# First up projection in 2x2 block products over half of the k-range, and modulation dots in the down projection

## The chip, the cores and the metric

The kernel runs on one core of a Trainium2 chip. A time is the device time of one execution in microseconds (us). The engines are TensorE (PE: matmuls; its weight loads are listed as PEld), VectorE (DVE), ScalarE (ACT), GpSimd (POOL) and SyncE (SP, which only issues transfers here). Transfers run on 16 DMA engines and are issued from the queues of SP, ACT and POOL.

## What is computed

One layer over 256 latent and 256 context tokens of width 2048, in f32: a half-step SwiGLU feed-forward (hidden width 5632) on both streams, token mixing (attention and a Hyena branch side by side), and a second half-step SwiGLU on the latent stream. Shift, scale and gate of each part come from a linear map of SiLU(c), nine chunks of 2048 columns each. Cut to what matters here:

```python
def swiglu(h, w_up, w_down):
    gate, up = jnp.split(h @ w_up, 2, axis=-1)
    return (jax.nn.silu(gate) * up) @ w_down

def half_ffn(s, m, slot, g, w_up, w_down):
    h = modulate(rms_norm(s, g), chunk(m, 3 * slot), chunk(m, 3 * slot + 1))
    return s + 0.5 * chunk(m, 3 * slot + 2) * swiglu(h, w_up, w_down)

mod   = silu(c)     @ w_ada + b_ada      # nine chunks, latent
mod_c = silu(c_ctx) @ w_ada + b_ada      # the same map, context
x   = half_ffn(x,   mod,   0, g_norm[0], w_ffn1_up, w_ffn1_down)
ctx = half_ffn(ctx, mod_c, 0, g_norm[0], w_ffn1_up, w_ffn1_down)
```

## The kernel before

**Tiles.** Activations are kept transposed: a k-tile is 128 features on the partitions and, on the free axis, 256 latent and 256 context tokens (2 x 256). There are 16 k-tiles of the width (KT) and 44 column tiles of the hidden width (JT; a column tile is called j). For precision every operand is split in two f32r parts, hi and lo, and `mm3` (L235) issues three matmuls for each product: hi x hi, hi x lo, lo x hi.

**Weights.** `weight` (L219) loads a raw tile of 128 x 1024 f32 (512 KB) from SP's queue into one of four "raw" slots, casts it to hi on ACT (L225) and subtracts to lo on DVE (L229). There are three slots each for hi ("whi") and lo ("wlo"). A raw slot is free once lo is made, a hi or lo slot once the last matmul that reads it is through.

**First up projection.** The first three j (WAVE) run beside the making of h. For j = 3 to 43 `Ffn.up` takes four pieces, one per quarter of the k-range: 4 k-tiles x (gate, up) x 3 matmuls of 512 columns. Two PSUM banks hold gate and up of one j; `close` (L372) applies SiLU on ACT, multiplies on DVE, splits the result and writes it to DRAM from POOL's queue. The h of all 16 k-tiles stays in SBUF in "u" tiles, 58 of which exist.

**Dots.** Chunk columns 2 to 8 of the modulation are made on DVE: `ada_dve` (L130) loads 128 columns x 1024 inputs (512 KB, four "adaw" slots, on SP's queue behind the newest weight load) and reduces them against SiLU(c) (L142); for chunks 2, 3 and 4 twice, with the context's as well. There are 7 x 16 x 2 = 224 such loads. After each piece a hook adds ADA_RATE = 1.375 to an account, and for each whole unit one load with its dots is issued. All are done when the up projection ends.

**First down projection.** `Ffn.down` (L414) makes three passes over 11 groups of four j: pass 0 and 1 with three double output tiles each, pass 2 with two. A step is one weight tile: 24 matmuls of 512. The act tiles of a group are fetched from DRAM on POOL's queue (`fetch`, L388) two groups ahead, up to five groups at a time; groups 9, 10 and 8 (the first of pass 0) are still in SBUF from the up projection. The last three groups of pass 2 are taken twice, with one half of the tokens each: 24 matmuls of 256 a step, context first, and the norm of the next stage runs beside the second half. The gate (chunk 2) is applied at the end of each pass.

The order of the instructions on each engine is written down when the program is built: a scheduler takes what is ready in its own estimate of times, earlier program text first, and each engine then runs its queue in that order.

Of the kernel before, what the change touches and what calls it, by code (L numbers as in the profile page):

```python
# [18 lines left out]
P = 128  # L19
D = 2048  # L20
# [11 lines left out]
WAVE = 3  # L32
ADA_RATE = 1.375
GT = JT // GRP
PASSES = ((0, 1, 2), (3, 4, 5), (6, 7))
ORDERS = ((9, 10, 8, 7, 6, 5, 4, 3, 2, 1, 0), tuple(range(GT)), tuple(reversed(range(GT))))
ROOM = 5
# [22 lines left out]
def hybrid_layer_kernel(ctx: ExitStack, tc: tile.TileContext, a):  # L60
# [288 lines left out]
    class Ffn:  # L349
        def __init__(self, wup, wdown, cm, hook=None):  # L350
            self.wup, self.wdown, self.cm = wup, wdown, cm
            self.hook = hook or (lambda: None)
            self.h = [None] * KT
            self.mm = mm3
            self.held = {}

        def open(self, alt=False):
            f = PB if alt else PA
            return f((P, 2, L)), f((P, 2, L))

        def piece(self, j, kq, ps2, w=None):
            w = w or weight(self.wup[j, kq], (P, 4, 2, P))
            for k4 in range(4):
                self.tile(kq * 4 + k4, k4, w, ps2)
            self.hook()

# [5 lines left out]
        def close(self, j, ps2):  # L372
            sg = tmp2((P, 2, L))
            S.activation(sg, ps2[0], AF.Silu)
            V.tensor_mul(sg, ps2[1], sg)
            act = split(sg, (P, 2, L))
            for s_ in range(2):
                nc.gpsimd.dma_start(actd[j][:, s_], act[s_])
            if j // GRP in ORDERS[0][0:3]:
                self.held.setdefault(j // GRP, []).append(act)  # L380

        def up(self, j, w=None):
            ps2 = self.open()
            for kq in range(4):
                self.piece(j, kq, ps2, None if kq else w)
            self.close(j, ps2)

# [25 lines left out]

        def down(self, before, between, after):  # L414

            uses = [(p, g) for p in range(len(PASSES)) for g in ORDERS[p]]
            for n, (p, g) in enumerate(uses):
# [17 lines left out]
                for dq in PASSES[p]:  # L435
                    self.hook()
                    self.step(g, dq, banks, g == ORDERS[p][0], g == ORDERS[p][-1] or at == -1)
            before()
            rest = [g for _, g in uses[-APART:]]
            for part in (1, 0):  # L440
# [5 lines left out]
                if part:  # L446
                    between()

# [113 lines left out]

    todo = [(c, d, b) for c in (2, 4, 3, 5, 7, 6, 8) for d in range(KT) for b in range(2)]
    owed = [0.0]

# [8 lines left out]
    def ada_hook():  # L574
        owed[0] += ADA_RATE
        while owed[0] >= 1.0:
# [193 lines left out]
    for _ in steps:  # L770
        pass
    ahead = weight(f1.wup[WAVE, 0], (P, 4, 2, P))
    for j in range(WAVE):
# [5 lines left out]

    xs = [[None] * (KT // 2) for _ in range(2)]  # L780
    for j in range(WAVE, JT):
        f1.up(j, ahead if j == WAVE else None)
        if j == WAVE:
            for i in range(2):
                crow.append(T(adap, (P, D), f"crow{i}", bufs=1))
                nc.scalar.dma_start(crow[i], a["crow"][i : i + 1, :].partition_broadcast(P))
                S.activation(crow[i], crow[i], AF.Silu)
            f1.hook = ada_hook
    while done[0] < len(todo):
        ada_next()  # L790
# [25 lines left out]
    f1.hook = lambda: None  # L816
    rs1 = U((P, 2, L))
    cont, lat = [], []

    def mix_input(i, out, early=None, bank=None):  # L820
        yield from rstd_steps(xs[i], D, rs1[:, i, :], early, bank)
        yield from normed_from(i, rs1[:, i, :], 3, out)

    more = mix_input(1, cont, PASSES[-1][0], PA)
    norm_plan = iter(NORM_PLAN)
    f1.down(lambda: next(more), lambda: next(more), lambda: [next(more) for _ in range(next(norm_plan))])


# [563 lines left out]
def _prepare(i):  # L1392
# [30 lines left out]
    d["cond"] = np.concatenate([pcol(i["b_ada"][0]).reshape(P, 9, KT), gn, cs], axis=1)  # L1423
    d["w_up1"] = pair(i["w_ffn1_up"][0], JT)
    d["w_dn1"] = down(i["w_ffn1_down"][0])
# [44 lines left out]
```

## Time and profile before

| | us |
|---|---|
| runs: median (lowest to highest) of 3 | 2661.37 (2660.85 to 2666.46) |
| the profiled execution | 2655.78 |
| its span, first to last instruction | 2653.9 |
| j = 4 to 43 of the first up projection | about 177 to 1050 |
| first down projection, pass 0 / 1 / 2 / the last steps | 1050 to 1230 / to 1410 / to 1497 / to 1532 |

The profile is of one execution; times in it are counted from the start of the span. A group's row has line, engine, operation, written and read tile, shapes and count, then the busy time and the mean duration of one in ns, then the idle time before it and what ended it. A matmul's record runs on after the next one has started, so its cost in a stream is read from the starts.

### The profile page before, as it was taken

Reading aid. Unit: us, or ns where it says so; the run is one execution under the profiler, and the core shown is the slowest. Engines: PE = TensorE matmul, PEld = TensorE weight load, DVE = VectorE, ACT = ScalarE, POOL = GpSimd, SP = SyncE. Lnnn points to the kernel's source line nnn. Section 1 sums busy time; section 2 is a strip of 40 time slices with the busy share of each in tenths; the row PEclk is TensorE's granted clock in tenths of the full one; section 3 lists DMA queues with packets and bytes.
Section 4 is the critical chain, followed back from the end, with each engine's and each line's share of the span. In section 5 each row is a group of like instructions: output and inputs, shape, how many; then the busy total and the mean of one; then the engine's idle time right before and its main releaser. Section 6 shows DMA issues by size and latency. Waiting matters only on the chain.

```text
span 2653.9 us, 32545 instructions
## 1 busy us (share of the span) xinstructions
PE 2630.5 (99%) x12434; PEld 2165.2 (82%) x12434; DVE 1606.4 (61%) x2393; ACT 930.4 (35%) x1208; POOL 152.8 (6%) x292
## 2 busy tenths in 40 slices
PE   8999999999999999999999999999999999999999
PEld 5678888788888888888888988888788888888887
DVE  6789999876665665223223496889665555554444
ACT  5332222222222222212112365456554444444333
POOL 1100000000000001410202100000000000000000
PEclk9999999999999999999999999999999999999999
DMA  9977767787777778953746555334555555556664
GB/s 366 362 263 254 253 237 263 232 282 258 253 258 248 260 251 273 345 159 127 224 133 209 190 172 191 122 132 162 173 182 191 190 190 189 188 188 206 204 199 159
DMA packets 178999, 579.75 MB, mean 218 GB/s; under 512 B 20635, under 2 KB 23644, under 8 KB 174492
## 3 DMA queue, kind: packets, MB, share of 16 engines
q1 hardware_dynamic: 139724, 500.72, 55.2%
q0 software_dynamic: 38496, 74.20, 9.5%
q10 hardware_dynamic: 624, 2.75, 0.3%
q8 instruction: 97, 1.59, 0.2%
q14 instruction: 58, 0.48, 0.1%
HBM read 550.32 MB, written 27.28 MB: 218 GB/s over the span
## 4 chain that ended last, share of the span: by engine, by line
PE 89%; DVE 5%; DMA 4%; issue 2%; ACT 0%; SPq 0%; DVEq 0%; ACTq 0%
PE pa L236 13%; PE pa L238 13%; PE pa L237 13%; PE pa L1132 10%; PE pa L1133 10%; PE pa L1134 10%; PE pb L236 3%; PE pb L237 3%; PE pb L238 3%; PE pa L244 3%; DMA adaw<-in_w_adaT_dram 2%; PE pa L246 2%; DVE adas L142 2%; DVE wlo L229 1%; PE pb L179 1%
## 5 line engine op out<-in xcount | busy, mean ns | idle before, releaser
L229 DVE TENSOR_TENSOR wlo<-raw,whi 128x1024 fp32r<-128x1024 f32 x637 | 779.4, 1224 | 793.3 <-ACT whi L225 769.7
L225 ACT CAST whi<-raw 128x1024 fp32r<-128x1024 f32 x637 | 670.0, 1052 | 1276.3 <-PE pa L237 561.4
L236 PE MATMUL pa<-u,whi 128*128 128x512 f32 (+1 forms) x1776 | 688.9, 388 | 2.1 <-ACT u L677 2.1
L238 PE MATMUL pa<-u,wlo 128*128 128x512 f32 (+1 forms) x1776 | 686.8, 387 | 2.2 <-DVE wlo L229 2.2
L237 PE MATMUL pa<-u,whi 128*128 128x512 f32 (+1 forms) x1776 | 686.7, 387 | 0.4 <-DVE u L682 0.4
L1132 PE MATMUL pa<-whi,u 128*128 128x512 f32 x1060 | 413.9, 391 | 0.0
L1133 PE MATMUL pa<-wlo,u 128*128 128x512 f32 x1060 | 412.8, 390 | 0.2 <-DVE wlo L229 0.2
L1134 PE MATMUL pa<-whi,u 128*128 128x512 f32 x1060 | 412.8, 390 | 0.0
L236 PEld LDWEIGHTS pa<-u,whi 128*128 128x128 f32 x1776 | 333.5, 188 | 75.2 <-issue 4.5
L238 PEld LDWEIGHTS pa<-u,wlo 128*128 128x128 f32 x1776 | 333.9, 188 | 70.9 <-DVE wlo L229 3.2
L237 PEld LDWEIGHTS pa<-u,whi 128*128 128x128 f32 x1776 | 333.9, 188 | 67.9 <-DVE u L682 1.5
L142 DVE CUSTOM_DVE_ANT_0 adas<-adaw,crow,cond 128x1024 bf16<-128x1024 f32 x160 | 205.2, 1282 | 51.3 <-DMA adaw<-in_w_adaT_dram 49.2
L142 DVE CUSTOM_DVE_ANT_0 adas<-adaw,crow,mod 128x1024 bf16<-128x1024 f32 x160 | 205.4, 1284 | 50.5 <-DMA adaw<-in_w_adaT_dram 47.3
L1134 PEld LDWEIGHTS pa<-whi,u 128*128 128x128 f32 x1060 | 199.0, 188 | 41.6
L1133 PEld LDWEIGHTS pa<-wlo,u 128*128 128x128 f32 x1060 | 199.1, 188 | 41.3 <-DVE wlo L229 0.6
L1132 PEld LDWEIGHTS pa<-whi,u 128*128 128x128 f32 x1060 | 199.0, 188 | 40.6
L236 PE MATMUL pb<-u,whi 128*128 128x512 f32 (+1 forms) x384 | 146.2, 381 | 0.0
L237 PE MATMUL pb<-u,whi 128*128 128x512 f32 (+1 forms) x384 | 144.5, 376 | 0.0
L238 PE MATMUL pb<-u,wlo 128*128 128x512 f32 (+1 forms) x384 | 144.4, 376 | 0.0
L244 PE MATMUL pa<-u,whi 128*128 128x512 f32 x384 | 137.4, 398 | 0.0
L395 POOL DMA_DIRECT2D u<-act x160 | 84.8, 550 | 337.7 <-PE pb L238 161.3
L246 PE MATMUL pa<-u,wlo 128*128 128x256 f32 x360 | 101.6, 283 | 0.0
(297 smaller groups left out, 2016.7 us busy)
## 6 DMA issues: line engine op xcount, KB each, us to landing
raw<-in_w_up_dram SPq DMA_DIRECT2D x340, 512.0 KB, 3.3
adaw<-in_w_adaT_dram SPq DMA_DIRECT2D x223, 512.0 KB, 5.6
raw<-in_w_dn_dram SPq DMA_DIRECT2D x182, 512.0 KB, 4.1
u<-act POOLq DMA_DIRECT2D x160, 256.0 KB, 6.1
wrow<-in_w_ada_dram SPq DMA_DIRECT2D x32, 1024.0 KB, 10.0
act<-u POOLq DMA_DIRECT2D x88, 256.0 KB, 5.4
raw<-in_w_hy_dram SPq DMA_DIRECT2D x32, 512.0 KB, 3.2
raw<-in_w_o_dram SPq DMA_DIRECT2D x32, 512.0 KB, 3.3
```

Of the source, the lines that this page charges most:

```text
L142: V.tensor_tensor_reduce(out=sc, in0=t, in1=crow[i][:, b * (D // 2) : (b + 1) * (D // 2)], scale=1.0, scalar=mcol if b else bada[:, n : n ...
L225: S.copy(hi, raw)
L229: V.tensor_sub(lo, raw, hi.bitcast(F32))
L236: PE.matmul(ps, w[0], xx[0], start=start, stop=False)
L237: PE.matmul(ps, w[0], xx[1], start=False, stop=False)
L238: return PE.matmul(ps, w[1], xx[0], start=False, stop=stop)
L244: PE.matmul(ps, w[0], x, start=start, stop=stop)
L246: PE.matmul(ps[:, 0, :], w[1], x[:, 0, :], start=False, stop=False)
L395: nc.gpsimd.dma_start(act[s_], actd[j][:, s_])
L1132: PE.matmul(ps[t], hi, w[0], start=start, stop=False)
L1133: PE.matmul(ps[t], hi, w[1], start=False, stop=False)
L1134: last = PE.matmul(ps[t], lo, w[0], start=False, stop=stop)
```

## The change

In the up projection the last quarter of the k-range is blocked from j = 4 on and the third quarter from j = 5 on (QUADS). A block product treats two k-tiles by two halves of the tokens (latent, context), and two k-tiles by gate and up, as 2x2 matrices and forms their product with seven products instead of eight. `combine` makes the sums and differences of h once for each pair of k-tiles and overwrites h's context half of the first k-tile; `prepare` makes those of the weights for each piece, in the raw tile, after the first three blocks are split (a tile of 768 columns) and before the other four are (1024 columns). A block piece is thus 2 pairs x 7 products x 3 = 42 matmuls of 256 columns. A j has four PSUM banks then, PA or PB in turn, and the end of `up` puts them together before SiLU.

The weights of j >= 3 lie in memory with their blocks in another order. The act tiles of the last groups are not kept in SBUF; the first group of the down projection is fetched during j = 43, the others in the usual way. Dots of chunks 5, 7, 6 and 8 are issued in the up projection (two loads a piece for j = 4 and 5, 0.7 a piece after that), those of chunks 2, 3 and 4 in the down projection, 1.27 loads a step. The pool that holds their tiles is given back after pass 2, and the constants of the mixing stage are loaded behind it.

```diff
@@ -30,10 +30,13 @@
 CT = HW // P
 EPS = 1e-6
 WAVE = 3
-ADA_RATE = 1.375
+ADA_UP = (5, 7, 6, 8)
+ADA_DOWN = (2, 3, 4)
+ADA_RATES = (2.0, 0.7, 1.27)
+QUADS = {3: 4, 2: 5}
 GT = JT // GRP
 PASSES = ((0, 1, 2), (3, 4, 5), (6, 7))
-ORDERS = ((9, 10, 8, 7, 6, 5, 4, 3, 2, 1, 0), tuple(range(GT)), tuple(reversed(range(GT))))
+ORDERS = ((9, 8, 10, 7, 6, 5, 4, 3, 2, 1, 0), tuple(range(GT)), tuple(reversed(range(GT))))
 ROOM = 5
 APART = 3
 NORM_PLAN = (0, 1, 0, 1, 0, 1, 1, 1, 1, 1, 1, 1)
@@ -353,16 +356,12 @@
             self.h = [None] * KT
             self.mm = mm3
             self.held = {}
+            self.sums = {}
+            self.wupq = a["w_up1q"]
 
         def open(self, alt=False):
             f = PB if alt else PA
             return f((P, 2, L)), f((P, 2, L))
-
-        def piece(self, j, kq, ps2, w=None):
-            w = w or weight(self.wup[j, kq], (P, 4, 2, P))
-            for k4 in range(4):
-                self.tile(kq * 4 + k4, k4, w, ps2)
-            self.hook()
 
         def tile(self, k, k4, w, ps2):
             for half in range(2):
@@ -373,17 +372,90 @@
             sg = tmp2((P, 2, L))
             S.activation(sg, ps2[0], AF.Silu)
             V.tensor_mul(sg, ps2[1], sg)
-            act = split(sg, (P, 2, L))
+            self.keep(j, sg)
+
+        def combine(self, kp):
+
+            (h0, l0), (h1, l1) = self.h[2 * kp], self.h[2 * kp + 1]
+            a0, a1, b0, b1 = tmp((P, 2, L)), tmp((P, 2, L)), tmp2((P, 2, L)), tmp2((P, 2, L))
+            V.tensor_add(a0, h0.bitcast(F32), l0.bitcast(F32))
+            V.tensor_add(a1, h1.bitcast(F32), l1.bitcast(F32))
+            V.tensor_add(b0[:, 0, :], a0[:, 1, :], a1[:, 1, :])
+            V.tensor_sub(b1[:, 0, :], b0[:, 0, :], a0[:, 0, :])
+            V.tensor_sub(b1[:, 1, :], a0[:, 1, :], a0[:, 0, :])
+            V.tensor_sub(b0[:, 1, :], a1[:, 0, :], b1[:, 0, :])
+            s23, s4 = split(b1, (P, 2, L)), U((P, 2, L), F32R)
+            split_to(b0[:, 0, :], h0[:, 1, :], l0[:, 1, :])
+            split_to(b0[:, 1, :], s4[:, 0, :], s4[:, 1, :])
+            self.sums[kp] = [(h0[:, 0, :], l0[:, 0, :]), (h1[:, 0, :], l1[:, 0, :]), (s4[:, 0, :], s4[:, 1, :]),
+                             (h1[:, 1, :], l1[:, 1, :]), (h0[:, 1, :], l0[:, 1, :]),
+                             tuple(t[:, 0, :] for t in s23), tuple(t[:, 1, :] for t in s23)]
+
+        def quads(self, j, kq):
+            return j >= QUADS.get(kq, JT)
+
+        def prepare(self, j, kq):
+
+            if not self.quads(j, kq):
+                return [weight(self.wupq[j - WAVE, kq], (P, 2, 4, P))]
+            raw = weight_load(self.wupq[j - WAVE, kq], (P, 2, 4, P))
+            out = []
+            for n in (3, 4):
+                if n == 4:
+                    V.tensor_sub(raw[:, :, 0:4:3], raw[:, :, 3:4].broadcast_to((P, 2, 2, P)), raw[:, :, 0:3:2])
+                    V.tensor_sub(raw[:, :, 2], raw[:, :, 2], raw[:, :, 0])
+                    V.tensor_sub(raw[:, :, 1], raw[:, :, 1], raw[:, :, 2])
+                hi, lo = T(wp, (P, 2, n, P), "whi", F32R, 3), T(wp, (P, 2, n, P), "wlo", F32R, 3)
+                out.append(split_to(raw[:, :, 0:n], hi, lo))
+            return out
+
+        def products(self, j, kq):
+
+            if not self.quads(j, kq):
+                for k4 in range(4):
+                    for half in range(2):
+                        yield half, None, 0, k4 // 2, (0, 1, 3, 2)[k4 % 2 + 2 * half], 4 * kq + k4
+                return
+            for n, terms in enumerate((((2, 0, 0, 0), (0, 0, 1, 1), (1, 0, 2, 2)),
+                                       ((0, 1, 1, 3), (3, 1, 0, 4), (2, 1, 2, 5), (3, 0, 3, 6)))):
+                for q in range(2):
+                    for bank, part, block, term in terms:
+                        yield bank, part, n, q, block, (2 * kq + q, term)
+
+        def up(self, j, w=None):
+            todo = [list(self.products(j, kq)) for kq in range(4)]
+            left = [sum(t[0] == bank for piece in todo for t in piece) for bank in range(4)]
+            total = list(left)
+            banks = [(PA, PB)[j % 2]((P, 2, L)) if n else None for n in left]
+            for kq in range(4):
+                w = w or self.prepare(j, kq)
+                for bank, part, n, q, block, x in todo[kq]:
+                    ps = banks[bank] if part is None else banks[bank][:, part, :]
+                    xx = self.h[x] if part is None else self.sums[x[0]][x[1]]
+                    left[bank] -= 1
+                    mm3(ps, [t[:, q, block] for t in w[n]], xx, left[bank] == total[bank] - 1, left[bank] == 0)
+                w = None
+                if j == JT - 1 and kq == 1:
+                    self.fetch(ORDERS[0][0])
+                self.hook()
+            if not total[2]:
+                return self.close(j, banks)
+            g, v, u = tmp((P, 2, L)), tmp2((P, 2, L)), T(up, (P, L), "mt", bufs=3)
+            S.copy(g[:, 0, :], banks[2][:, 0, :])
+            V.tensor_add(u, g[:, 0, :], banks[2][:, 1, :])
+            V.tensor_add(g[:, 1, :], u, banks[3][:, 0, :])
+            V.tensor_add(v[:, 0, :], u, banks[3][:, 1, :])
+            V.tensor_add(v[:, 1, :], g[:, 1, :], banks[3][:, 1, :])
+            V.tensor_add(g, g, banks[0])
+            V.tensor_add(v, v, banks[1])
+            S.activation(g, g, AF.Silu)
+            V.tensor_mul(v, v, g)
+            self.keep(j, v)
+
+        def keep(self, j, act):
+            act = split(act, (P, 2, L))
             for s_ in range(2):
                 nc.gpsimd.dma_start(actd[j][:, s_], act[s_])
-            if j // GRP in ORDERS[0][0:3]:
-                self.held.setdefault(j // GRP, []).append(act)
-
-        def up(self, j, w=None):
-            ps2 = self.open()
-            for kq in range(4):
-                self.piece(j, kq, ps2, None if kq else w)
-            self.close(j, ps2)
 
         def fetch(self, g):
 
@@ down @@
-        def down(self, before, between, after):
+        def down(self, after):
 ...
-            before()
+            yield
             rest = [g for _, g in uses[-APART:]]
 ...
                 if part:
-                    between()
+                    yield
 ...
@@ -560,8 +632,8 @@
                     yield
 
 
-    todo = [(c, d, b) for c in (2, 4, 3, 5, 7, 6, 8) for d in range(KT) for b in range(2)]
-    owed = [0.0]
+    todo = [(c, d, b) for c in ADA_UP + ADA_DOWN for d in range(KT) for b in range(2)]
+    owed, rate = [0.0], [0.0]
 
     def ada_next():
         if done[0] < len(todo):
@@ -572,7 +644,7 @@
                 ada_finish(c, d, d + 1)
 
     def ada_hook():
-        owed[0] += ADA_RATE
+        owed[0] += rate[0]
         while owed[0] >= 1.0:
             owed[0] -= 1.0
             ada_next()
@@ -769,7 +841,7 @@
                 raws = [weight_load(f1.wup[j, d // 4 + 1], (P, 4, 2, P), G) for j in range(WAVE)]
     for _ in steps:
         pass
-    ahead = weight(f1.wup[WAVE, 0], (P, 4, 2, P))
+    ahead = f1.prepare(WAVE, 0)
     for j in range(WAVE):
         f1.close(j, wave[j])
     rowp_cm.__exit__(None, None, None)
@@ -778,14 +850,31 @@
     crow = []
 
     xs = [[None] * (KT // 2) for _ in range(2)]
+    ready = {j: kq for kq, j in QUADS.items()}
     for j in range(WAVE, JT):
+        if j in ready:
+            for kp in (2 * ready[j], 2 * ready[j] + 1):
+                f1.combine(kp)
         f1.up(j, ahead if j == WAVE else None)
+        rate[0] = ADA_RATES[j >= 5]
         if j == WAVE:
             for i in range(2):
                 crow.append(T(adap, (P, D), f"crow{i}", bufs=1))
                 nc.scalar.dma_start(crow[i], a["crow"][i : i + 1, :].partition_broadcast(P))
                 S.activation(crow[i], crow[i], AF.Silu)
             f1.hook = ada_hook
+    rs1 = U((P, 2, L))
+    cont, lat = [], []
+
+    def mix_input(i, out, early=None, bank=None):
+        yield from rstd_steps(xs[i], D, rs1[:, i, :], early, bank)
+        yield from normed_from(i, rs1[:, i, :], 3, out)
+
+    more = mix_input(1, cont, PASSES[-1][0], PA)
+    norm_plan = iter(NORM_PLAN)
+    rate[0] = ADA_RATES[2]
+    downs = f1.down(lambda: [next(more) for _ in range(next(norm_plan))])
+    next(downs)
     while done[0] < len(todo):
         ada_next()
     last_load[0] = None
@@ after the kspec loads @@
-    more = mix_input(1, cont, PASSES[-1][0], PA)
-    norm_plan = iter(NORM_PLAN)
-    f1.down(lambda: next(more), lambda: next(more), lambda: [next(more) for _ in range(next(norm_plan))])
+    next(more)
+    next(downs)
+    next(more)
+    for _ in downs:
+        pass
 ...
@@ -1421,7 +1504,10 @@
     d["w_ada1"] = np.stack([w.reshape(2, 8, P, 2 * P).transpose(0, 2, 1, 3) for w in blocks])
     gn = i["g_norm"][0].reshape(3, KT, P).transpose(2, 0, 1)
     d["cond"] = np.concatenate([pcol(i["b_ada"][0]).reshape(P, 9, KT), gn, cs], axis=1)
-    d["w_up1"] = pair(i["w_ffn1_up"][0], JT)
+    w = pair(i["w_ffn1_up"][0], JT)
+    d["w_up1"] = c_(w[:WAVE])
+    w = w[WAVE:].reshape(JT - WAVE, 4, P, 2, 4, P)
+    d["w_up1q"] = c_(w[:, :, :, :, [0, 2, 3, 1], :])
     d["w_dn1"] = down(i["w_ffn1_down"][0])
     w = i["w_ffn2_up"][0].reshape(8, 2, P, 2, UPG, 256)
     d["w_up2"] = c_(w.transpose(4, 0, 2, 1, 3, 5)).reshape(UPG, 8, P, 2, 512)
```

More of the change, by code (lines that the diff above doesn't have):

```diff
@@ L816, in hybrid_layer_kernel @@
     f1.hook = lambda: None
[L817 to L822, printed above, removed]
-    more = mix_input(1, cont, PASSES[-1][0], PA)
-    norm_plan = iter(NORM_PLAN)
-    f1.down(lambda: next(more), lambda: next(more), lambda: [next(more) for _ in range(next(norm_plan))])
+    next(more)
[3 more added lines that the diff above has]
+        pass
     def proj_cols(w, ttiles, hook=lambda: None):
```

## Prediction

> **What bounds the kernel now.** I read the page first, then the windows by stage, then the order of single instructions in one stage.
>
> ```profile
> span 2653.9 us, 32545 instructions
> PE 2630.5 (99%) x12434; PEld 2165.2 (82%) x12434; DVE 1606.4 (61%) x2393; ACT 930.4 (35%) x1208; POOL 152.8 (6%) x292
> ...
> PE   8999999999999999999999999999999999999999
> PEld 5678888788888888888888988888788888888887
> DVE  6789999876665665223223496889665555554444
> ...
> PE 89%; DVE 5%; DMA 4%; issue 2%; ACT 0%; SPq 0%; DVEq 0%; ACTq 0%
> ```
>
> The reader is to see that TensorE (PE) is busy in every slice and makes 89% of the chain that ended last: time goes only if TensorE gets less work, and comes back if it has to wait. VectorE (DVE) is the next: nine tenths in slices 4 to 7, six tenths in the rest of the first up projection, two in the down projection (slices 17 to 22).
>
> ```profile
> 160.00:420.00 260.00, 260.00 (x1148) 215.29 (x1148) 239.13 (x399) 65.92 (x74) 13.36 (x26) 1.00 0.77 260
> 177.40:1050.00 872.60, 870.44 (x3839) 720.05 (x3838) 648.82 (x970) 210.17 (x240) 42.65 (x80) 1.00 0.76 256
> 1050.00:1230.00 180.00, 180.00 (x796) 149.10 (x795) 46.69 (x46) 37.12 (x37) 41.34 (x78) 1.00 0.69 222
> 1080.00:1110.00 30.00, 30.00 (x134) 24.84 (x133) 6.70 (x6) 5.28 (x5) 11.90 (x23) 1.00 1.19 388
> 1498.00:1514.00 16.00, 16.00 (x136) 16.00 (x135) 8.51 (x10) 5.96 (x7) 0.00 (x0) 1.00 0.49 165
> ```
>
> These are windows: length, busy PE, weight loads, DVE, ACT, POOL, granted clock, DMA share, GB/s. From 160 to 420 us DVE is 92% busy (239.13 of 260) and PE loses nothing. In the whole stretch of column tiles j = 4 to 43 (177.4 to 1050) PE lacks 2.2 us, and the waits (engine, what it waited for, us in all, times, longest) name them:
>
> ```profile
> PE pa L238 <- DVE wlo L229: 2.2, 2, 1.3
> DVE adas L142 <- DMA adaw<-in_w_adaT_dram: 96.5, 85, 3.8
> ```
>
> **Step 1, the products.** Two sets of starts on PE: matmuls 512 wide in the up projection (first and last of 57), and 256 wide at the end of the down projection (first and last of 24, the shape of the new block products).
>
> ```profile
> 214.69 0.39 PE L237 MATMUL pa<-u,whi 128*128 128x512 f32 x1
> ...
> 227.38 0.39 PE L236 MATMUL pa<-u,whi 128*128 128x512 f32 x1
> ...
> 1514.44 0.28 PE L236 MATMUL pb<-u,whi 128*128 128x256 f32 x1
> ...
> 1517.20 0.28 PE L238 MATMUL pb<-u,wlo 128*128 128x256 f32 x1
> ```
>
> A 512-wide matmul costs 12.69 / 56 = 0.2266 us, a 256-wide one 2.76 / 23 = 0.120 us: more than half. An old piece (a quarter of the k-range of one j) is 4 k-tiles x 2 halves x 3 = 24 matmuls of 512: 5.44 us. A block piece is 2 pairs x 7 products x 3 = 42 of 256: 5.04 us. The eighth saved becomes 7%: 0.40 us. The last quarter is blocked from j = 4 (40 pieces), the third from j = 5 (39): 79 x 0.40 = **31.6 us less**. The margin is thin: at 5.44 / 42 = 0.1295 us a matmul the gain is gone.
>
> Weight loads (PEld) rise from 24 to 42 a piece. In the window 1498 to 1514 they are busy 16.00 of 16.00 us, and the spacing is still 0.120 there, so I take 0.120. [...]
>
> **Step 2, the added VectorE and ScalarE work.** Durations of one, by shape:
>
> ```profile
> L229 DVE TENSOR_TENSOR wlo<-raw,whi 128x1024 fp32r<-128x1024 f32 x637 | 779.4, 1224 | 793.3 <-ACT whi L225 769.7 <-DMA adaw<-in_w_adaT_dram 7.4 <-DMA u<-in_xT_dram 4.2
> L142 DVE CUSTOM_DVE_ANT_0 adas<-adaw,crow,mod 128x1024 bf16<-128x1024 f32 x160 | 205.4, 1284 | 50.5 <-DMA adaw<-in_w_adaT_dram 47.3
> L201 DVE TENSOR_TENSOR u<-sg,u 128x512 fp32r<-128x512 f32 x44 | 30.1, 684 | 0.0
> L375 DVE TENSOR_TENSOR sg<-pa,sg 128x512 f32<-128x512 f32 x43 | 29.6, 689 | 36.7 <-PE pa L238 36.7
> L142 DVE DVE_READ_ACCUMULATOR2_ANT mod<- 128x1 f32 x320 | 26.5, 83 | 0.0
> L950 DVE TENSOR_TENSOR sg<-pa,sg 128x256 f32<-128x256 f32 x24 | 9.6, 422 | 4.9 <-ACT sg L949 4.9
> ...
> L225 ACT CAST whi<-raw 128x1024 fp32r<-128x1024 f32 x637 | 670.0, 1052 | 1276.3 <-PE pa L237 561.4 <-PE pa L1134 413.4 <-PE pb L237 169.6
> L200 ACT CAST u<-sg 128x512 fp32r<-128x512 f32 x44 | 27.4, 622 | 107.1 <-DVE sg L375 107.1
> ```
>
> From j = 6 on, one j needs of DVE: two plain splits 2 x 1.22; two block pieces, each a split of 768 (between 0.68 and 1.22, middle 0.95), one subtraction of 512 (0.68), two of 256 (0.84), a split of 1024 (1.22), so 3.7 each; the longer close with 4 operations of 256 and 4 of 512, 4.4; 0.7 x 4 = 2.8 dots at 1.28 + 0.08, 3.8. That is 18.1 us in 2 x 5.44 + 2 x 5.04 = 20.96: 86%, under the 92% above. ACT needs casts of 2 x 1.05 + 2 x 1.89 + 0.62 and two operations of like size for the close, some 7.5 us. So throughput is no bound; the order is. The splits now go through three whi/wlo slots in six uses a j instead of four. A slot comes free when the item three back ends. Before, that left 2 x 5.44 us for 1.05 + 1.22 us of work: 8.6 us of slack. Now the worst item is the 1024 split of the last block piece: its slot opens when the first tile of the block piece before is used up, and 24 and 18 matmuls later (5.04 us, 4.84 without the 0.16 that a 256-wide matmul runs on after the next one starts) it is due. The 768 split before it, whose slot opens 2.16 us earlier (18 matmuls), takes ACT 0.84 (middle of 0.62 and 1.05) and DVE 0.95, then the three subtractions 1.52: they end 1.15 us into those 4.84. ACT 1.05 and DVE 1.22 follow: **slack about 1.4 us**. One dot ahead of it on DVE's queue (1.37) uses that up. Bounds: nothing, if the 2.8 dots fall into the start of the j; one dot too many in every second j, some 0.4 us a time, 8 us. I take 4 us.
>
> At the start: the sums of h cost per pair of k-tiles 3 x 0.69 + 6 x 0.42 = 4.6, four pairs 18.4 us, and j = 4 and 5 each carry 8 dots, 21.9 us together. With weights (7.4 + 9.9) and closes (1.4 + 4.4) DVE has 63.4 us to do in 21.36 + 20.96 of PE and some 13 us left over in j = 3: 8 us too much, pushed into j = 6 to 8, which have 2.9 us spare each. The dots feed nothing on PE here, but stand in the same queue. Bounds 0 and 8; I take 2. The sums overwrite half of h once the last plain piece has read it; 16 us (j = 4) and 11 us (j = 5) remain until they are used.
>
> PSUM: four banks a j, of alternating tags, are closed in one whole j: 0. The act tiles written anyway and fetched again: the fetch of the first group starts half a j ahead and U tiles come free with each quarter: 0, covered by 5 us of that j.
>
> **Step 3, the dots in the down projection.** 122 of the 224 chunk loads stay in the up; 102 move to the 82 steps of the down, with two dots each. DVE per step: 1.22 + 1.27 x 2 x 1.37 = 4.7 of 5.44 us, 86%, and here the slack of the splits is still 8.6 us: 0. The loads are the tight part. Pass 0 before:
>
> ```profile
> DMA packets 17006, 40.01 MB, mean 222 GB/s; under 512 B 1884, under 2 KB 1884, under 8 KB 16997
> ...
> u<-act POOLq DMA_DIRECT2D x76, 256.0 KB, 6.7
> raw<-in_w_dn_dram SPq DMA_DIRECT2D x33, 512.0 KB, 3.3
> ...
> kspec<-spec SPq DMA_DIRECT2D x16, 128.0 KB, 3.3
> ...
> 662.17 0.38 SPq L138 DMA_DIRECT2D adaw<-in_w_adaT_dram  x1
> ```
>
> To these come 33 x 1.27 = 42 chunks of 0.52 MB and 16 fetches of 0.26 MB: 66.2 MB in 180 us, 368 GB/s, against 388 in the window 1080 to 1110, where PE didn't wait. If 388 is the limit, pass 0 needs 171 of its 180 us: 0; if the pass can't do better than its 0.69 share a 222 GB/s (322), 206 us: 26 more. I take 2 us, as the nearest row is the 388 one. [...] Issuing costs SP 1.27 x 0.38 = 0.5 us more a step, and POOL, 41.34 of 180 us busy in pass 0, the 16 fetches: 0, both queues mostly stand idle. The 16 loads of kspec and 8 smaller ones need the room of the chunks, so they wait for the last dot and come at about 1490 instead of at the start of pass 0: 24 x 0.38 = 9 us on SP's queue, ahead of the raw tiles of the last steps (24 x 0.120 = 2.88 us each): 0 while four raw tiles lie loaded (11.5 us), 9 with none; I take 0, as the queue was as full at the start of pass 0 and PE didn't wait. Chunk 2 is through after 30 of the 33 steps of pass 0, at whose end it is used; chunk 4 after 80 of 82 steps, and the first norm uses it after half of the last steps, 17 us later.
>
> Sum: -31.6 + 4 + 2 + 2 = **-23.6 us**. The profiled execution took 2655.78 us (1.9 beside its span), 5.6 below the median of 2661.37; on the median that makes **2638 us**.
>
> **Rivals.**
> (a) All waits are hidden: -28 to -32, 2629 to 2633. For it: 92% DVE without a wait. Against: the slack goes from 8.6 to 1.4.
> (b) Slower: DVE's queue holds a dot that waits for its chunk between the two splits of the last block piece. Its price: a mean wait of 96.5 / 85 = 1.14, plus 1.37, less the slack of 1.4: 1.1 us, and more where the wait is longer (3.8 is the longest). It decides from 31.6 / 39 = 0.81 us a j; at 1.4 us in every j, 55 us: 2685, at 1.1 us 2673. For it: the chunk is asked for right behind the raw tile, and lands 5.6 us (median) later, about when the last piece is prepared. Against: only one chunk in 2.8 has that place.
>
> ```profile
> DMA to landing us min/median/max: 3.6/5.6/10.3
> ```
>
> (c) Transfers bound pass 0 of the down projection, by up to the 26 us of step 3: 2636 to 2662, the middle 2649. For it: 368 of 388 GB/s. Against: the prefetch of two groups, and 388 without a wait. [...]
> (d) The change doesn't do what it says, since the block products don't come at 0.120: at 0.1295 a matmul nothing changes, 2661; were each load (188 ns) bare, 42 x 0.308 against 5.44 is 7.5 us more a piece, 3250. [...] Against both: 24 starts in a row at 0.120.
>
> ```profile
> L236 PEld LDWEIGHTS pa<-u,whi 128*128 128x128 f32 x1776 | 333.5, 188 | 75.2 <-issue 4.5
> ```
>
> **Chances.** Forecast (4 to 20 us of waits, 2634 to 2650) 0.42; (a) 0.26; (c) 0.10, of it 0.03 within 0.2%; (b) 0.16; (d) 0.06, half within 0.2% and half slower, the bare loads next to nothing of it. 0.2% is 5.3 us, about what a measurement can tell. Faster 0.42 + 0.26 + 0.07 = 0.75, same 0.06, slower 0.19. The range reaches from below (a), 2626, to the edge of no change, 2662, and leaves out the slower cases.
>
> **What would show it.** Matmuls of 256 at 0.120 us apart in the up, and that stage near 841 instead of 872.6 us (1); PE waits on DVE's wlo of a few us in all, at the first matmul of a block piece's second half (2); PE without waits and DMA near 1.1 in pass 0 (3). Wrong: waits of PE on wlo over 30 us, or a down projection longer than before.

## The result and the profile after

The changed kernel takes 2682.89 us (median; 2681.42 to 2687.43) where the kernel before takes 2661.11 in the same comparison: ratio 1.0081, 95% interval 1.0063 to 1.0100. It is slower by 0.8%, where 0.9% faster was predicted. The profiled execution took 2687.43 us (span 2685.6, before 2653.9): 31.7 us more in the span. One run of e9 below took 3688.66 us at a mean granted clock of 0.655 and is left out of its time and ratio.

The page of the kernel after: span, engines, busy tenths of 40 slices, granted clock, and the chain that ended last.

```profile
span 2685.6 us, 36384 instructions
PE 2625.9 (98%) x13856; PEld 2219.3 (83%) x13856; DVE 1897.1 (71%) x2985; ACT 1018.8 (38%) x1339; POOL 165.5 (6%) x316
...
PE   8999999999999998999999999999999999999999
...
DVE  5788878877787876678778497789765555554444
...
PEclk8999999999999998999999999999999999999999
...
PE 77%; DMA 10%; DVE 9%; issue 3%; ACT 1%; SPq 0%; DVEq 0%; ACTq 0%
```

PE is busy for 4.6 us less than before (2625.9 against 2630.5) in a span that is 31.7 us longer, so it is idle for 36.3 us more. DMA and DVE have 19% of the chain, before 9%. Slice 16 (1007 to 1074 us), the end of the up projection and the start of the down projection, shows PE and its clock below nine tenths.

Windows of after by stage (length, busy PE, weight loads, DVE, ACT, POOL, granted clock, DMA share, GB/s):

```profile
200.00:220.00 20.00, 16.78 (x87) 13.72 (x86) 20.00 (x39) 6.71 (x12) 1.07 (x2) 0.99 0.64 225
220.00:240.00 20.00, 16.78 (x88) 14.98 (x88) 17.98 (x29) 5.30 (x7) 0.14 (x1) 0.84 0.53 185
...
300.00:1000.00 700.00, 700.00 (x4390) 636.05 (x4389) 558.86 (x883) 246.08 (x300) 36.26 (x68) 1.00 0.57 195
1020.00:1050.00 30.00, 25.84 (x143) 23.20 (x142) 22.90 (x38) 8.85 (x11) 7.87 (x15) 0.89 0.90 295
1050.00:1100.00 50.00, 43.09 (x164) 32.80 (x164) 33.06 (x57) 6.49 (x7) 22.25 (x42) 0.86 1.14 379
1100.00:1500.00 400.00, 381.80 (x1637) 310.71 (x1635) 309.16 (x489) 75.84 (x75) 64.63 (x122) 0.98 0.86 292
```

From 300 to 1000 us, the bulk of the block products, PE waits for nothing. It is idle for 6.4 us at 200 to 240, 4.2 at the end of the up, 6.9 at the start of the down and 18.2 in the rest of it, each time with a lower granted clock as well (0.84 to 0.99). The starts of matmuls mark the stages: the up ends at about 1037.6 (before 1050.6), and the last steps begin at 1528.82 (before 1497.16). So the up is 13.0 us shorter, and the down from there 491.2 us long in place of 446.5, 44.7 longer; 44.7 - 13.0 = 31.7. The same stretch of the down, before and after:

```profile
1050.60:1497.16 446.56, 446.56 (x1971) 369.87 (x1970) 117.86 (x119) 91.37 (x91) 85.83 (x162) 1.00 0.64 202
```

```profile
1037.60:1528.80 491.20, 464.45 (x1970) 375.89 (x1969) 364.42 (x580) 90.67 (x92) 94.31 (x178) 0.97 0.89 302
```

For the same matmuls PE is busy 17.9 us longer, at a granted clock of 0.97, and idle for 26.8 us: these are the 44.7. Two fifths of the loss are thus slower matmuls and not waiting; the last section shows the one beside the other.

The waits of DVE (1020 to 1500 us) and of PE (1020 to 1510 us): us in all, times, longest.

```profile
DVE adas L145 <- DMA adaw<-in_w_adaT_dram: 95.2, 43, 8.7
```

```profile
PE pb L241 <- DVE wlo L232: 9.3, 7, 2.2
PE pa L241 <- DVE wlo L232: 6.4, 3, 4.2
PE pa L240 <- DMA u<-act: 4.7, 4, 1.5
PE pb L241 <- DVE wlo L209: 4.2, 1, 4.2
PE pb L241 <- DVE mod L156: 4.0, 1, 4.0
PE pa L239 <- DMA u<-act: 2.2, 3, 0.8
```

Most of PE's waits are for a split that DVE made late (the one put down to mod, which ends at 1132.17, too: a split ends on DVE at 1132.11), and DVE's own waits are mostly for chunks, the loads of the dots. The longest stop of PE there in order of time, DVE first, then ACT, then PE:

```profile
1314.70 1.22 DVE L232 TENSOR_TENSOR wlo<-raw,whi 128x1024 fp32r<-128x1024 f32 x1
1320.44 1.29 DVE L145 CUSTOM_DVE_ANT_0 adas<-adaw,crow,mod 128x1024 bf16<-128x1024 f32 x1 [4.52 <-DMA adaw<-in_w_adaT_dram]
1321.65 0.08 DVE L145 DVE_READ_ACCUMULATOR2_ANT mod<- 128x1 f32 x1
1321.77 1.28 DVE L145 CUSTOM_DVE_ANT_0 adas<-adaw,crow,mod 128x1024 bf16<-128x1024 f32 x1
...
1323.10 1.28 DVE L145 CUSTOM_DVE_ANT_0 adas<-adaw,crow,cond 128x1024 bf16<-128x1024 f32 x1
...
1324.43 1.28 DVE L145 CUSTOM_DVE_ANT_0 adas<-adaw,crow,cond 128x1024 bf16<-128x1024 f32 x1
...
1325.64 1.22 DVE L232 TENSOR_TENSOR wlo<-raw,whi 128x1024 fp32r<-128x1024 f32 x1
```

```profile
1316.60 1.05 ACT L228 CAST whi<-raw 128x1024 fp32r<-128x1024 f32 x1 [5.24 <-PE pb L240]
```

```profile
1326.91 0.80 PE L241 MATMUL pa<-u,wlo 128*128 128x512 f32 x1 [4.23 <-DVE wlo L232]
```

ACT has the hi part ready at 1317.65. The split that makes the lo part starts at 1325.64, 8.0 us later: ahead of it on DVE's queue stand four dots, and the first waits 4.52 us for its chunk. PE pays 4.23 us of that.

### The profile page after: what moved, and what is told of

It reads as the page before. It is cut to its first block, busy times and chain, and to the rows that moved or that the text cites. A ratio compares the mean times of both kernels' runs of the same rounds, so it can differ in the third digit from the quotient of the medians.

```text
span 2685.6 us, 36384 instructions
## 1 busy us (share of the span) xinstructions
PE 2625.9 (98%) x13856; PEld 2219.3 (83%) x13856; DVE 1897.1 (71%) x2985; ACT 1018.8 (38%) x1339; POOL 165.5 (6%) x316
## 4 chain that ended last, share of the span: by engine, by line
PE 77%; DMA 10%; DVE 9%; issue 3%; ACT 1%; SPq 0%; DVEq 0%; ACTq 0%
PE pa L1216 10%; PE pa L1217 10%; PE pa L1215 10%; DMA adaw<-in_w_adaT_dram 8%; PE pb L241 6%; PE pa L239 6%; PE pb L239 6%; PE pa L240 6%; PE pb L240 6%; PE pa L241 6%; PE pa L247 3%; DVE adas L145 3%; DVE wlo L232 2%; PE pa L249 2%; PE pb L182 1%
## 5 line engine op out<-in xcount | busy, mean ns | idle before, releaser
L232 DVE TENSOR_TENSOR wlo<-raw,whi 128x1024 fp32r<-128x1024 f32 x558 | 681.5, 1223 | 436.4 <-ACT whi L228 434.8
L241 PE MATMUL pa<-u,wlo 128*128 128x512 f32 (+1 forms) x1338 | 461.9, 345 | 6.5 <-DVE wlo L232 6.4
L239 PE MATMUL pa<-u,whi 128*128 128x512 f32 (+1 forms) x1338 | 463.8, 347 | 4.3 <-DMA u<-act 2.2
L240 PE MATMUL pa<-u,whi 128*128 128x512 f32 (+1 forms) x1338 | 462.2, 346 | 5.1 <-DMA u<-act 4.7
L241 PE MATMUL pb<-u,wlo 128*128 128x512 f32 (+1 forms) x1296 | 445.4, 344 | 18.4 <-DVE wlo L232 9.6
L239 PE MATMUL pb<-u,whi 128*128 128x512 f32 (+1 forms) x1296 | 445.3, 344 | 4.4 <-ACT whi L208 3.5
L240 PE MATMUL pb<-u,whi 128*128 128x512 f32 (+1 forms) x1296 | 443.7, 343 | 1.2 <-DVE u L209 1.2
L241 PEld LDWEIGHTS pb<-u,wlo 128*128 128x128 f32 x1296 | 249.0, 193 | 51.2 <-DVE wlo L232 18.6
L239 PEld LDWEIGHTS pa<-u,whi 128*128 128x128 f32 x1338 | 255.4, 191 | 41.5 <-issue 4.5
L240 PEld LDWEIGHTS pa<-u,whi 128*128 128x128 f32 x1338 | 255.5, 191 | 36.7 <-DMA u<-act 6.4
L239 PEld LDWEIGHTS pb<-u,whi 128*128 128x128 f32 x1296 | 248.7, 192 | 33.8 <-ACT whi L208 3.9
L240 PEld LDWEIGHTS pb<-u,whi 128*128 128x128 f32 x1296 | 248.9, 192 | 29.2 <-DVE u L209 1.5
L208 ACT CAST whi<-raw 128x768 fp32r<-128x768 f32 (+1 forms) x158 | 148.8, 943 | 245.3 <-DVE raw L407 169.7
L209 DVE TENSOR_TENSOR wlo<-raw,whi 128x768 fp32r<-128x768 f32 (+1 forms) x158 | 171.7, 1089 | 89.8 <-ACT whi L208 87.3
```

Of the source, the lines that this page charges most:

```text
L208: S.copy(hi, src)
L209: V.tensor_sub(lo, src, hi.bitcast(F32))
L232: V.tensor_sub(lo, raw, hi.bitcast(F32))
L239: PE.matmul(ps, w[0], xx[0], start=start, stop=False)
L240: PE.matmul(ps, w[0], xx[1], start=False, stop=False)
L241: return PE.matmul(ps, w[1], xx[0], start=False, stop=stop)
```

## The experiments

Theories named in the expectations: V, the dots' work on VectorE alone; L, the chunk transfers alone; F, the late fetch of act tiles; S, the overload at the start of the up; W, work and waits in order on VectorE's queue; R, chunks asked for too late; O, the order of that queue; B, transfers set the pace wherever things stand. The code cuts below are shortened, marked by + and - against the changed kernel (e4: against the kernel before). Ratios are to the kernel before, run beside them on the same chip (2661.11 us beside after, 2657.7 to 2658.2 beside the others).

| run | us | ratio (95%) |
|---|---|---|
| after | 2682.89 | 1.0081 (1.0063 to 1.0100) |
| e1 no dots in the down | 2647.51 | 0.9959 (0.9944 to 0.9974) |
| e2 dots, no loads | 2642.90 | 0.9941 (0.9924 to 0.9957) |
| e3 loads, no dots | 2651.38 | 0.9979 (0.9970 to 0.9988) |
| e4 before, dots moved | 2682.28 | 1.0092 (1.0076 to 1.0108) |
| e5 group 10 held | 2671.77 | 1.0047 (1.0029 to 1.0065) |
| e6 five chunk buffers | 2681.83 | 1.0087 (1.0071 to 1.0103) |
| e7 no overload at the start | 2679.24 | 1.0077 (1.0061 to 1.0093) |
| e8 fewer dots in the down | 2648.14 | 0.9964 (0.9950 to 0.9978) |
| e9 loads two dots ahead | 2677.28 | 1.0071 (1.0054 to 1.0088) |
| e10 products, dots in the up | 2741.47 | 1.0315 (1.0294 to 1.0336) |
| e11 even, ahead, held | 2643.72 | 0.9947 (0.9933 to 0.9962) |
| e12 the same, more in the up | 2640.14 | 0.9935 (0.9918 to 0.9951) |
| e13 dots behind the splits | 2646.44 | 0.9960 (0.9945 to 0.9974) |
| e14 ahead, behind the splits | 2637.28 | 0.9933 (0.9916 to 0.9950) |
| e15 e12, behind the splits | 2631.90 | 0.9906 (0.9891 to 0.9921) |

### The moved dots: work, loads, or both (e1 to e4)

```diff
 e1: the dots and loads of chunks 2, 3, 4 are left out (their columns are set to 0.5)
-ADA_DOWN = (2, 3, 4)
+ADA_DOWN = ()
 e2: those dots read a tile that lies in SBUF, and nothing is loaded for them
-out=sc, in0=t, in1=crow[i][:, here]
+out=sc, in0=crow[1 - i][:, here], in1=crow[i][:, here]
 e3: the chunks are loaded, and of each only a column is read
+if c in ADA_DOWN:
+    V.tensor_scalar(mcol, t[:, i : i + 1], 0.5, None, op0=ALU.mult)
+    continue
 e4: the kernel before with ADA_UP, ADA_DOWN, ADA_RATES and the split `down` of the change, no block products
```

> The changed kernel without the dots of chunks 2, 3 and 4: neither their 96 loads nor their 192 dots are there, the three chunks are set to 0.5. The changed kernel takes 2683 us: its first up projection from j = 4 on is 13 us shorter than before, its down projection 45 us longer. Theory L (the chunk loads fill the DMA engines in the down projection, and act fetches, weight tiles and VectorE's queue wait on them): the down projection goes back to nearly 447 us up to its last steps, and the time to 2640 to 2650. Theory V (the dots fill VectorE's queue ahead of the weight splits): the same. Theory F (the fetches of the three groups that were held in SBUF before): the down projection keeps 20 us or more, 2660 to 2683.

> The changed kernel with all dots of chunks 2, 3 and 4, but on a tile that already lies in SBUF: their 96 loads are left out, VectorE has the same work. Theory L: as without dots, 2640 to 2650. Theory V: 2675 to 2683, as the changed kernel. Theory F: 2660 to 2683, no better than without the dots.

> The changed kernel with all its 96 chunk loads in the down projection, but instead of a dot of 128 x 1024 VectorE only reads one column of the tile (two operations of 128 x 1 for a load). Theory L: most of the 45 us of the down projection stays, 2670 to 2683, if act fetches and weight tiles are what comes late; 2655 to 2665 if it takes both the late load and a full VectorE behind it. Theory V: 2640 to 2650.

> The kernel before (no block products, acts of groups 9, 10 and 8 held in SBUF), with the order and the rates of dots of the changed kernel: chunks 5, 7, 6, 8 in the up projection, 2, 3, 4 in the down projection at 1.27 loads a step. Theories L and V: the down projection is 25 to 45 us longer, 2686 to 2706. Theory F: nothing but noise, 2656 to 2666, as the three groups are held.

The same 380 us of the down in e1, e2, e3 and after:

```profile
1100.00:1480.00 380.00, 380.00 (x1678) 314.67 (x1677) 98.93 (x99) 77.64 (x76) 64.08 (x121) 1.00 0.61 195
```

```profile
1100.00:1480.00 380.00, 380.00 (x1678) 314.76 (x1677) 301.27 (x477) 77.70 (x76) 59.83 (x113) 1.00 0.62 197
```

```profile
1100.00:1480.00 380.00, 380.00 (x1679) 314.74 (x1678) 118.91 (x321) 77.64 (x76) 67.94 (x129) 1.00 0.92 317
```

```profile
1100.00:1480.00 380.00, 363.27 (x1559) 296.29 (x1558) 298.32 (x470) 71.64 (x71) 56.90 (x108) 0.98 0.84 287
```

In this window work alone costs PE nothing (DVE 301 of 380 us busy), transfers alone cost nothing (317 GB/s, more than in after), and both together cost 16.7 us of idle PE. Over the whole down up to the last steps e1 takes 454.1 us, e2 450.2 and e3 458.8, against 446.5 before and 491.2 in after. So V and L both fall as single causes, and so does F, since e1 and e2 keep the fetches. By the times e2 lies in L's range, far from V's, and e3 lies 1.4 us above V's range, below both of L's. e4 shows the same loss without a block product (363.38 us of the 380 busy): the moved dots alone make the old kernel 0.92% slower, some 4 us less than its range said.

### Smaller losses and the share of dots (e5 to e8)

```diff
 e5: the act tiles of group 10 stay in SBUF
-ORDERS = ((9, 8, 10, 7, 6, 5, 4, 3, 2, 1, 0), tuple(range(GT)), tuple(reversed(range(GT))))
+ORDERS = ((9, 10, 8, 7, 6, 5, 4, 3, 2, 1, 0), tuple(range(GT)), tuple(reversed(range(GT))))
+            if j // GRP == ORDERS[0][1]:
+                self.held.setdefault(j // GRP, []).append(act)
 e6: five buffers
-t = T(adap, (P, D // 2), "adaw", bufs=4)
+t = T(adap, (P, D // 2), "adaw", bufs=5)
-return T(up, shape, "u", dt, 58)
+return T(up, shape, "u", dt, 56)
 e7 and e8: rates
-ADA_RATES = (2.0, 0.7, 1.27)
+ADA_RATES = (0.76, 0.76, 1.27)
+ADA_RATES = (0.9, 0.9, 1.0)
```

> The changed kernel, but the act tiles of group 10 (the last four column tiles of the up) stay in SBUF when they are made, and the down takes the groups in the order 9, 10, 8, 7 ... instead of 9, 8, 10, 7 ...; so the second group needs no fetch and group 8 has 16 us more until it is wanted. Theory F (the late fetch of group 8, seven PE waits on 'u<-act' at 1056 to 1067 us and the low clock up to 1073, is a separate loss of 7 to 14 us): 2668 to 2676, and no PE wait on 'u<-act' near 1056. Theory W (VectorE's queue in the down sets the pace anyway: 4.7 us of work and about 1.2 us of waiting for chunks in steps of 5.44): the time saved is taken back by later waits for 'wlo', 2678 to 2685.

> The changed kernel with five buffers for the chunks in place of four (the room comes from the pool of 2 KB tiles, 56 in place of 58). Theory W with the wait as a matter of prefetch depth: the chunk is asked for one dot earlier (about 2.2 to 4 us), VectorE's 95 us of waits on 'adaw' in the down fall below 35 us, so work and waits fit in the step: 2652 to 2665. Rival B (the chunks land late because the queues are full, 6.5 us median where the up had 5.3, and one more outstanding only lengthens the landing): waits stay over 70 us, 2675 to 2686.

> The changed kernel with dot rates of 0.76 per piece through the whole up, in place of 2.0 for j = 4 and 5 and 0.7 after; the down keeps 1.27 per step. Theory S (the sums of h and the double rate of dots in j = 4 and 5 overload VectorE at 200 to 240 us: PE idle 6.4 us and about 3 us of low clock): 2672 to 2677, PE over 95% busy at 220 to 240. Rival: the sums of h alone fill VectorE there, so the loss stays: 2680 to 2686. No theory has the down move.

> The changed kernel with dot rates of 0.9 per piece in the up and 1.0 per step in the down (1.27 before): VectorE's work per step of the down falls from about 4.7 to about 4.1 us, the chunk loads in the down by a fifth. Theory W (in order: work and waits summed against 5.44 us): 4.1 + 1.2 = 5.3 fits just, the down loses most of its 35 us and the start some of its 9: 2638 to 2652. Theory V (VectorE's work alone decides): the same or better. Theory L (chunk transfers alone decide): a fifth less traffic gives a fifth of the 35 us, 2670 to 2678.

e5 wins 0.34%, as F said: at 1050 to 1100 PE is busy for 50.00 of 50 us at full clock, where after has 43.09 at 0.86. e6 changes nothing: DVE waits 93.7 us for chunks (40 times) against 95.2, so W's reading as a matter of depth failed, and the time lies in B's range. e7 removes the stop at 220 to 240 (PE busy 20.00, clock 1.00): its up ends at 1031.0, 6.7 us earlier than in after, and its down takes 491.2 us as there. Its median is only 3.7 us lower and misses S's range by 2 us (the intervals of the ratios overlap). e8 wins 1.2%, in the range of W and V and not of L, yet DVE still waits 93.7 us for chunks there: with less work in the step the waits fit, they don't go.

### When the chunk is asked for, and where the dots can go (e9 to e12)

```diff
 e9: in ada_next, each load is written two dots ahead of its dots
+            while asked[0] < min(done[0] + 3, len(todo)):
+                ada_load(*todo[asked[0]])
+                asked[0] += 1
             ada_dve(c, d, b)
 e10: all seven chunks from the start of the up
+ADA_UP, ADA_DOWN, ADA_RATES = (2, 3, 4, 5, 7, 6, 8), (), (1.375, 1.375, 1.375)
 e11, e12: as e9, group 10 held, and a chunk of two dots counts two
-while owed[0] >= 1.0:
-    owed[0] -= 1.0
+while done[0] < len(todo) and owed[0] >= 1 + (todo[done[0]][0] < 5):
+    owed[0] -= 1 + (todo[done[0]][0] < 5)
+ADA_RATES = (0.7, 1.0, 2.0)
+ADA_RATES = (0.7, 1.1, 1.8)
```

> The changed kernel, same dots at the same places, but each chunk's load is written two dots earlier, so it stands two places further ahead among the weight loads on SP's queue; four buffers as before. Theory R (a chunk's load is chained behind the weight loads on SP, each of which waits for the split of four steps earlier, so it is asked for only about one step, 5 us, ahead of its dot and lands in 6.1: VectorE's 95 us of waits are a matter of when the load is asked for): waits on 'adaw' in the down below 35 us, the dots' 4.7 us then fit in the step of 5.44, the down loses 25 to 35 us, 2648 to 2660. Rival B (transfers set the pace in the down: landing grows with what is outstanding): waits over 70 us, 2672 to 2685.

> The changed kernel's block products with the dots as in the kernel before: all seven chunks from the up's start at 1.375 per piece (chunks 2, 4, 3 of two dots each come first), hardly any in the down. Worked from the profile of after: pieces of 5.24 us on the mean, VectorE 0.80 busy with 0.7 dots of 1.36 us, so 3.24 us a piece without them. While the double chunks last (96 / 1.375 = 70 pieces) it needs 3.24 + 1.375 x 2.72 = 6.98 us: 70 x 1.74 = 122 us lost; after them 5.11, just covered. Against 2683 the down wins back its 45: 2740 to 2790. Theory 'PE's time alone counts' : 2683 - 45 = 2638, down to 2620.

> The changed kernel with what the runs so far point to: dots counted by their work (a chunk of 2, 3, 4 counts two), 0.7 a piece for j = 4 and 5, 1.0 a piece after, 2.0 a step in the down (that is 1.0 double chunks, as in the run with fewer dots in the down); chunk loads asked for two dots ahead; act tiles of group 10 held. Against that run's 2648: the end of the up (PE idle 5.5 us and some low clock at 1020 to 1050, VectorE 93% busy there with double chunks at 0.9) wins 5 to 8, the fetches of 1050 to 1100 2, the waits of 1100 to 1200 5 to 7: 2630 to 2640. Rival: what is left there is the queue's transfers (1.18 busy DMA share, 393 GB/s at 1050 to 1100) and stays: 2642 to 2650.

> As the even run, with 1.1 a piece in the up and 1.8 a step in the down: VectorE at 3.24 + 1.5 = 4.74 of 5.24 us in the up, about 1.25 + 2.45 = 3.7 of 5.44 in the down. If the down was still short of VectorE's time, 1 to 5 below the even run; if the up's slack is the tighter one, 2 to 8 above it.

e9 came out in B's range, 5.6 us below after, and its waits for chunks stayed at 85.7 us: as it was built, R failed, and after e6 and e9 rival B stood, until e13. e10 agrees with the sum of work, at the lower edge of its range: with the products and the old place of the dots, DVE is busy for 673 of the 700 us from 300 to 1000 and PE for 652. So the up has no room for all the dots, and the moved dots are the price of the products. e11 misses its range and lands in the rival's, though not for the rival's reason: at 1050 to 1100 PE is busy for 50.00 of 50 us there with 394 GB/s. e12 is 3.6 us below it, as expected where the down is still short of VectorE's time; its down is 2.8 us shorter.

What e6 and e9 have in common is seen in the order in which DVE's instructions stand in the built programs. For each dot, from the first weight of the down on, count the splits that are written ahead of it in the program text and yet stand behind it on DVE's queue; and in the last column those splits behind it whose weight tile stands ahead of its chunk on SP's queue:

| kernel | dots | splits passed, mean | splits of tiles asked for ahead of its chunk, mean |
|---|---|---|---|
| after, e6 | 197 | 2.81 (161 dots pass three) | 2.81 |
| e9 | 197 | 4.31 | 2.75 |
| e4 | 197 | 2.94 | 2.94 |
| e13 | 197 | 0.08 | 0.87 |
| e14 | 197 | 0.13 | 0.88 |
| e15 | 146 | 0.00 | 0.00 |

The scheduler takes a dot ahead of three splits that are not ready in its estimate. More buffers (e6) leave that order as it was. When the load is written earlier (e9), it moves the dot earlier too, so the dot stands as close behind its load as before. That led to the next runs.

### The order on VectorE's queue (e13 to e15)

```diff
 e13 (e14: with e9's loads; e15: on e12); last_split is the tensor_sub of the newest `weight`
+            with ExitStack() as order:
+                if c < 5 and last_split[0] is not None:
+                    order.enter_context(tc.issue_after(last_split[0].ins))
                 V.tensor_tensor_reduce(
```

> The changed kernel with every dot of chunks 2, 3, 4 held on VectorE's queue behind the split that was written before it, so no dot stands ahead of a split of an earlier step; chunk loads are written where they were. Theory O (order: hoisted dots wait for chunks just asked for, and the splits of weights that have landed stand behind them): the waits for chunks in the down fall from 95 to below 50 us and what remains delays only the next step's split, 2655 to 2670. Rival B (transfers set the pace, the wait comes back wherever the dot stands): waits over 70 us, 2674 to 2686.

> Both: chunk loads written two dots earlier and the dots held behind the split written before them, so that a chunk has two dots' distance (about 8 us) more than it had. Theory O: waits for chunks below 25 us, 4.7 us of work fit in 5.44, the down loses nearly all of its 35 us, while the start and the late fetch of group 8 stay: 2645 to 2658. Rival B: 2670 to 2684.

> The best version so far (even dots with more of them in the up, two ahead, group 10 held: 2640) with the dots of chunks 2, 3, 4 held behind the splits. Theory O: PE's 5 us of waits for 'wlo' at 1100 to 1200 go, 2632 to 2638. Rival: with 1.8 dots a step those waits are slack already, 2638 to 2643.

The 380 us of the down in e13, and DVE's waits in it:

```profile
1100.00:1480.00 380.00, 380.00 (x1678) 314.64 (x1677) 316.20 (x502) 77.66 (x76) 69.78 (x132) 1.00 0.94 318
```

```profile
DVE wlo L235 <- ACT whi L231: 54.3, 45, 1.7
DVE tab L982 <- DMA qkg<-in_qkg_dram: 7.3, 1, 7.3
DVE u L484 <- PE pa L244: 0.3, 2, 0.2
```

The same dots, loads and buffers as in after, in another order on DVE's queue (on SP's queue 78 of the 222 chunk loads stand one or two weight loads later with it, none earlier): no wait for a chunk is left in this window (after has 78.1 us in it), PE is busy throughout with more transfers (318 GB/s) and more work of DVE than in after, and the time falls by 1.2% of the kernel before. Theory O holds, B falls; e13 and e14 both come out some 8 us better than O's ranges, in part since the late fetch costs less, too (at 1050 to 1100 PE is busy for 47.41 us in e13 and 49.19 in e14, 43.09 in after). From the end of the up to the last steps, e13 takes 453.6 us, e14 448.1, e15 446.5, before 446.5, after 491.2. e15, at the lower edge of its range, ends at 2631.90, 0.94% below the kernel before; at the start it still has 5.1 us of idle PE (200 to 300).

## Why the prediction was wrong

**Step 1, the products (-31.6): right.** Block products come 0.120 us apart (6.11 us for 51 of them) beside 91% busy weight loads (636.05 of 700). Rival (d) is out.

```profile
643.33 0.28 PE L239 MATMUL pb<-u,whi 128*128 128x256 f32 x1
...
649.44 0.28 PE L239 MATMUL pb<-u,whi 128*128 128x256 f32 x1
```

**Step 2, the steady state (+4, bounds 0 and 8): right, a little better.** PE loses nothing from 300 to 1000 us with DVE at 80%; the slack of 1.4 us was enough, and rival (b) didn't occur where it was placed, but for the last piece of the last j: there a dot waits 4.24 us for its chunk ahead of the last split, and PE 4.16 us for that split, up to 1033.40.

**Step 2, the start (+2, bounds 0 and 8): mis-sized.** PE idles 6.4 us at 200 to 240 and has 0.84 of its clock in the second half: by estimate 6.4 + 0.16 x 20 = 9.6 us. The 8 us of overload were taken as deferred; they stopped PE at once. From 214 to 220 us it waits for the sums of h themselves and for what DVE makes behind them; its longest stop, 2.67 us up to 228.64, is for a hi part whose three subtractions stand among the dots on DVE's queue. e7, with fewer dots there, is left with 1.7 us of idle PE.

**The act tiles written and fetched again (0): wrong.** The fetch of the second group is late: at 1050 to 1100, 6.9 us of idle PE and by estimate 0.14 x 43.1 = 6 us of clock, 13 together. e5 bought 0.34%, 9 us, of it back.

**Step 3, the dots in the down: the step that failed.** It set 4.7 us of work against 5.44 (86%) with "the slack of the splits is still 8.6 us: 0". The work was right: e2 and e13 run it without a wait of PE from 1100 to 1480. But the slack was DVE's busy time set against the step; it left out that a dot can wait on the queue with splits behind it. Dots stood ahead of 2.8 splits on the mean and waited for their chunks: over 82 steps 95.2 / 82 = 1.2 us a step, and 4.7 + 1.2 = 5.9 exceeds 5.44 by 0.4 us, some 35 us in all. From 1100 to 1480 DVE is busy for 298.3 us and waits 78.1 for chunks, 376.4 of 380: there was no slack left. After's down is 44.7 us longer; without the 13 of the late fetch that is 32, against the 35 of this sum. The prediction named a longer down as a sign of being wrong, and that came; its other sign, over 30 us of waits on wlo, did not (19.9 us from 1020 us on, 23.9 with the stop put down to mod). It was the mechanism of rival (b), given 0.16, priced there 2673 to 2685; it was weighed against the block pieces alone and not against the down, so that the time fell into its price is chance. The row that would have warned was quoted: 85 waits for chunks of 1.14 us on the mean in the kernel before, in a stretch where PE lost only 2.2 us in all.

**Step 3, the transfers (+2, bounds 0 and 26): about right.** e3 moves the same loads at 317 GB/s without a wait of PE in the 380 us, so rival (c) is not the cause of the long down. They do cost something at the first fetches: at 1050 to 1100 PE is busy for 43.17 us in e3 and for 47.37 in e1, which has no such loads, and e3 takes 3.9 us more in all.

By the stages: at the end of the up PE idles 4.2 us and loses by estimate 0.11 x 25.8 = 2.8 of clock, 7 together; -31.6 + 9.6 + 7 gives -15 for the up, measured -13. e14, with the dots and loads the change has and an order that lets them run, comes to 2637.28, next to the 2638 that was forecast for a down without waits; some of that is chance, since e14 also shortens the end of the up (PE busy 28.4 of 30 us at 1020 to 1050).

Not settled: whether e4 too would be mended by the order, which wasn't tried.

## What to carry to other kernels

On an engine that runs its queue in order, add an instruction's wait to its work, and ask what stands behind it: 86% busy with 1.2 us of waits a step was over 100%. When a scheduler fills a gap with work that waits for a transfer, neither more buffers nor an earlier request need help: here the first left the order as it was, and with the second the work moved along. Pin the work behind what the critical engine needs, and look at the queue's order before counting bytes. Undo work and transfers singly first: here each alone cost 4 to 12 us of the down, and both together 45.

## What the runs showed of the hardware

In after, two stops of PE cost more than their length. After the stop of 3.97 us that ended at 1132.17, matmuls of 512 columns come 0.43 us apart, and the granted clock is half from 1131.0, before the stop ends, to 1137.9:

```profile
1132.17 0.80 PE L241 MATMUL pb<-u,wlo 128*128 128x512 f32 x1 [3.97 <-DVE mod L156]
1132.76 0.63 PE L239 MATMUL pb<-u,whi 128*128 128x512 f32 x1
1133.19 0.63 PE L240 MATMUL pb<-u,whi 128*128 128x512 f32 x1
...
1137.88 0.39 PE L239 MATMUL pb<-u,whi 128*128 128x512 f32 x1
```

```profile
1128.00:1132.00 4.00, 0.20 (x1) 0.00 (x0) 3.61 (x5) 0.61 (x1) 1.07 (x3) 0.88 1.10 397
...
1134.00:1136.00 2.00, 2.00 (x6) 1.57 (x5) 1.96 (x3) 0.00 (x0) 1.34 (x4) 0.50 1.21 412
...
1138.00:1140.00 2.00, 2.00 (x11) 1.61 (x10) 0.62 (x4) 0.07 (x1) 0.58 (x2) 1.00 1.16 384
```

The 5.7 us at half speed cost about 2.9 us more (an estimate, half of them). The stop of 4.23 us that ended at 1326.91 did the same for 5.3 us. With seven stops of 0.7 to 1.5 us between 1055 and 1067 the clock was half as well, from 1059.4 to 1073.0. Two stops of 1.96 us differ: after the one that ended at 1171.15 the spacing was 0.43 for 3 us from 1172.3 on, after the one at 1475.95 it stayed 0.23.

The clock records in the trace of after give the stretches at half clock. The four that begin in the down do so at 1059.4, 1131.0, 1172.0 and 1325.6 us and last 13.65, 6.83, 3.41 and 6.83 us. Their beginnings lie 71.7, 41.0 and 153.6 us apart, 21, 12 and 45 times the shortest of them, and the others last four and two times as long as it. There is no such stretch at the stop that ended at 1475.95; what made the difference between the two stops of 1.96 us is not shown.
